# A feed-forward product by seven block products instead of eight, with a separate second product

## The chip, the cores and the metric

The kernel runs on one core of a Trainium2 chip. The core has five engines with queues of their own: TensorE (PE, matmuls; its weight loads are listed apart as PEld), VectorE (DVE), ScalarE (ACT), GpSimd (POOL) and SyncE (SP, which here only issues transfers). Within a queue, instructions start in order; between engines they wait on semaphores. Data lies in DRAM, in SBUF (128 partitions) or in PSUM, where PE accumulates its products in tiles of 128 x 512 float32. The metric is device time in microseconds (us); lower is better.

## The reference

One trunk layer on 1024 tokens of width 1024, in float32: windowed attention heads and gated-DeltaNet heads read one normalised input, their joined output is projected and added to the input, and a feed-forward block with a squared ReLU follows. The change is in the feed-forward part and in the place where it begins:

```python
h = h + jnp.concatenate([attn, gdn], axis=-1) @ w_out[l]
hn = _rmsnorm(h, norm_ffn_w[l])
h = h + jnp.square(jax.nn.relu(hn @ w_ffn_in[l])) @ w_ffn_out[l]
...
return _rmsnorm(h, norm_final_w)
```

`w_ffn_in` is 1024 x 4096 and `w_ffn_out` 4096 x 1024.

## The kernel before

**Arithmetic.** A float32 product is made of three matmuls on rounded halves of the operands. `split` (L112) writes the rounded value h with an ACT cast (L115) and the rest l with a subtraction on POOL (L116). `mm3` (L118) then accumulates h x h, h x l and l x h (L120, L121, L122) into one PSUM tile. Each matmul takes a 128 x 128 stationary block and 512 columns of the moving operand. A `gemm` (L253) runs it over eight blocks of 128 of the contraction: 24 matmuls.

**Buffers.** All SBUF tiles come from tagged pools with a fixed number of buffers: pg (28 of 4 KB per partition), pt (12 of 2 KB), sc and wr (4 each of 4 KB), wh and wl (3 each of 4 KB). PSUM has two tags, psA and psB, of 4 tiles each. A new tile of a tag waits until a buffer of that tag has been read for the last time. The order of each engine's queue is set when the kernel is built, by a planner (`schedule_with_timeline_sim`, L1116) that lists the instructions by their place in the program and by when it expects them to be ready. `weave` (L51) interleaves two generators in the program by the costs that they yield, divided by a weight.

**The stages before the feed-forward part.** Projections, then attention together with the two scans of the DeltaNet, then the output projection. `output` in `phases` (L1068) runs the attention, `out_attn`, the loading of the first group of `w_ffn_in` (`load_w1(0)`, two wr buffers, 512 KB each) and `out_all` (L911), which goes through the eight token chunks from the last to the first. For each chunk, `out_gdn` (L886) takes two wr buffers (`mix` and `zc`), loads the gate with L890, scales (L902), transposes on PE (L905), multiplies (L906) and splits; `out_gemm` multiplies by `w_out` (24 matmuls) and adds to `h[c]` on DVE (L871). h stays in eight pg buffers until the end of the kernel. `norm_h` (L926) makes a chunk's normalised rows in sc buffers (ACT square L199, POOL L186 and L187, DVE L201).

**The feed-forward part.** Tokens are taken in two halves of 512. `hn_half` (L934) transposes a half's rows in eight blocks (four PE transposes each, L205) and splits each block with one ACT instruction (L210) and one DVE instruction (L211) into a pg buffer. The second half is made while the projection ends; the first half beside the first 48 matmuls of `ffn1` on the second half. The hidden features go in 16 groups of 256. For a group, `ffn1` (L957) computes four tiles (two blocks of 128 features, two token halves; 24 matmuls each), with the squared ReLU on ACT and DVE (L964, L965) and a split of the result by ACT and POOL (L966, L967) into pg buffers. `ffn2` (L971) uses these as the stationary operand: for each of eight token chunks and two halves of the output, six matmuls into psB and one DVE addition into h (L983). In the loop of `phases`, `ffn1` of group g + 1 is put ahead of `ffn2` of group g; weights are loaded and split a group ahead (`load_w1` L940, `load_w2` L944). In the last group `finish` (L1000) normalises and stores the rows.

Of the kernel before, what the change touches and what calls it, by code (L numbers as in the profile page):

```python
# [9 lines left out]
F32 = mybir.dt.float32  # L10
# [53 lines left out]
def run(gen):  # L64
    for _ in gen:
        pass
# [7 lines left out]
class Block:  # L74
# [43 lines left out]
    def mm3(self, ps, wh, wl, xh, xl, first, last):  # L118
        nc = self.nc
        nc.tensor.matmul(ps, wh, xh, start=first, stop=False)  # L120
        nc.tensor.matmul(ps, wh, xl, start=False, stop=False)  # L121
        nc.tensor.matmul(ps, wl, xh, start=False, stop=last)  # L122
# [788 lines left out]
    def out_all(self, chunks):  # L911
# [3 lines left out]
        for n, c in enumerate(chunks):  # L915
# [4 lines left out]
            yield from self.out_gemm(self.h[c], *ready.pop(0), self.wo[1])  # L920
            self.summed.append(c)
# [12 lines left out]
    def hn_half(self, half):  # L934
        self.norm_half(half)
        yield 0.5
        self.hnt[half] = []
        yield from self.transpose_split([self.rows[4 * half + i] for i in range(4)], self.w_ffn, "psB", self.hnt[half])

    def load_w1(self, g):  # L940
        raws = self.load_w(self.w_cols(self.io["w_ffn_in"][0], 256 * g, 256))
        return [self.split_w(raws, lambda r: r[:, :, i * P:(i + 1) * P]) for i in range(2)]

    def load_w2(self, g):  # L944
        out = []
        for i in range(2):
            raw = self.wr((P, D))
            r = (2 * g + i) * P
            self.nc.sync.dma_start(out=raw, in_=self.io["w_ffn_out"][0, r:r + P, :])
            h, l = self.sc(dt=F32R), self.sc(dt=F32R)  # L950
# [6 lines left out]
    def ffn1(self, w1, out, order):  # L957

        nc = self.nc
        for i, half in order:  # L960
            a = self.pg((P, 2, HALF), F32R)
            ps = self.gemm(w1[i], self.hnt[half], "psA")
            r, q = self.pt(), self.pt()
            nc.scalar.activation(out=r, in_=ps, func=AF.Relu)  # L964
            nc.vector.scalar_tensor_tensor(out=q, in0=ps, scalar=0.0, in1=r, op0=ALU.max, op1=ALU.mult)  # L965
            nc.scalar.copy(out=a[:, 0], in_=q)  # L966
            nc.gpsimd.tensor_tensor(out=a[:, 1], in0=q, in1=a[:, 0].bitcast(F32), op=ALU.subtract)  # L967
            out[i, half] = a
            yield 5.2

    def ffn2(self, a, w2, tiles, last):  # L971
        nc = self.nc
        for t in tiles:
            tk = slice(t % 4 * P, (t % 4 + 1) * P)
# [3 lines left out]
            for nh, sl in enumerate(halves):  # L978
                ps = self.ps("psB")
                for i in range(2):  # L980
                    at = a[i, t // 4]
                    self.mm3(ps, at[:, 0, tk], at[:, 1, tk], w2[i][0][:, sl], w2[i][1][:, sl], i == 0, i == 1)
# [27 lines left out]
    def build(self):  # L1010
        tc, nc = self.tc, self.nc
        with (
# [6 lines left out]
            self.biasd = d("biasd", (8, 32, 512))[:]  # L1019
            self.gcd = dram.tile([3, 64, P], BF16, name="gcd")[:]  # L1020
# [7 lines left out]
    def phases(self):  # L1028
# [38 lines left out]

        def output():  # L1068
            yield from self.attention()
            yield from self.out_attn()  # L1070
            self.w1 = self.load_w1(0)
# [3 lines left out]
            yield from weave((out, 20.0), (self.hn_half(1), 12.0))  # L1075
# [7 lines left out]
        a, w1 = {}, self.w1  # L1083
        self.norm_half(0)
        run(weave((self.ffn1(w1, a, ((0, 1), (1, 1))), 10.0), (self.hn_half(0), 12.0)))
        run(self.ffn1(w1, a, ((0, 0), (1, 0))))
        w1, w2 = self.load_w1(1), self.load_w2(0)
        for g in range(ng):
            if g + 1 < ng:
                nxt = {}  # L1090
                run(self.ffn1(w1, nxt, ((0, 1), (0, 0), (1, 1), (1, 0))))
                if g + 2 < ng:
                    w1 = self.load_w1(g + 2)
                else:
                    self.w_fin = self.wh((P, D), F32)
                    nc.sync.dma_start(out=self.w_fin, in_=self.io["norm_final_w"].unsqueeze(0).to_broadcast([P, D]))
# [23 lines left out]
```

## Time and profile before

| | |
|---|---|
| median of 3 runs | 1331.63 us (1328.95 to 1333.94) |
| the profiled execution | 1328.63 us |
| its span, first to last instruction | 1326.6 us |
| mean granted TensorE clock | 0.99 |
| transfers | 120.48 MB, mean 91 GB/s |

The profile is of one execution. Busy time is how long an engine had an instruction in flight; for PE, whose matmuls overlap one another, the distance between starts tells the rate and the duration of one matmul doesn't. A row of grouped instructions reads: line, engine, operation, output <- inputs by the names of their buffers, shape, count | busy us, mean ns of one | idle time of the engine before them and what ended it. A row of a stage (A:B, us from the span's start) lists the busy time and the instructions of PE, PEld, DVE, ACT and POOL where these are shown, then the granted clock, the busy share of the DMA engines and GB/s. A row in order of time begins with the start and the duration.

### The profile page before, as it was taken

The numbers are of one execution on the slowest core, as the hardware profiler recorded it, in microseconds if no ns is written. First come the engines' busy times: TensorE is split into PE (matmuls) and PEld (weight loads), VectorE is DVE, ScalarE is ACT, GpSimd is POOL, SyncE is SP. The second block draws the span as 40 slices with busy tenths as digits, with TensorE's granted clock in tenths as the row PEclk, the third lists the DMA queues.
The fourth block names the chain that finished last, engine by engine and source line by source line (L and its number), as shares of the span: only waits on it lengthen the run. The fifth ranks groups of instructions, "written<-read, shape, count | busy, mean of one in ns | idle before, by whom it ended". The sixth has DMA issues, their size and how long they took to land.

```text
span 1326.6 us, 18332 instructions
## 1 busy us (share of the span) xinstructions
PE 1291.2 (97%) x6866; PEld 1041.0 (78%) x6866; DVE 649.7 (49%) x1339; ACT 469.8 (35%) x1085; POOL 460.9 (35%) x432
## 2 busy tenths in 40 slices
PE   7999998999899999999999999999999999999997
PEld 5788876877677778888888888888888888888885
DVE  5667676862689875754223322332233223322336
ACT  6454787244756731235221122112211221122113
POOL 5364122433432251443433133323332333233223
PEclk9999998998899999999999999999999999999999
DMA  6143455315666773120221122012201220122003
GB/s 225 61 133 108 119 174 190 104 48 139 158 173 175 225 284 114 56 72 18 79 64 32 32 64 65 27 37 64 64 19 46 64 64 17 48 64 64 16 1 127
DMA packets 85913, 120.48 MB, mean 91 GB/s; under 512 B 7075, under 2 KB 60448, under 8 KB 85825
## 3 DMA queue, kind: packets, MB, share of 16 engines
q1 hardware_dynamic: 77124, 114.82, 27.2%
q0 software_dynamic: 8448, 4.20, 1.7%
q8 instruction: 54, 0.88, 0.3%
q14 instruction: 34, 0.28, 0.1%
q10 hardware_dynamic: 253, 0.30, 0.1%
HBM read 88.84 MB, written 29.93 MB: 90 GB/s over the span
## 4 chain that ended last, share of the span: by engine, by line
PE 71%; DVE 1%; DMA 0%; issue 0%; ACT 0%; POOLq 0%; POOL 0%; SPq 0%; DVEq 0%; ACTq 0%
PE psA L120 11%; PE psA L121 11%; PE psA L122 11%; PE psB L121 9%; PE psB L120 9%; PE psB L122 9%; PE psB L792 4%; PE psA L580 2%; PE psA L569 1%; PE psA L540 1%; PE psA L541 1%; PE psB L205 0%; DMA pg<-in_w_out 0%; PE psB L756 0%; PE psA L905 0%
## 5 line engine op out<-in xcount | busy, mean ns | idle before, releaser
L120 PE MATMUL psA<-pg,wh 128*128 128x512 f32 x864 | 343.4, 399 | 2.3 <-ACT pt L454 2.1
L121 PE MATMUL psA<-pg,wh 128*128 128x512 f32 x864 | 343.2, 398 | 0.0
L122 PE MATMUL psA<-pg,wl 128*128 128x512 f32 x864 | 343.0, 398 | 0.0
L983 DVE TENSOR_TENSOR pg<-pg,psB 128x512 f32<-128x512 f32 x256 | 175.5, 687 | 277.3 <-PE psB L122 275.9
L116 POOL TENSOR_TENSOR wl<-wr,wh 128x512 fp32r<-128x512 f32 x108 | 152.7, 1435 | 282.4 <-ACT wh L115 282.2
L121 PE MATMUL psB<-sc,pg 128*128 128x512 f32 x512 | 202.5, 396 | 0.0
L120 PE MATMUL psB<-sc,pg 128*128 128x512 f32 x512 | 201.2, 394 | 0.0
L122 PE MATMUL psB<-sc,pg 128*128 128x512 f32 x512 | 200.8, 392 | 0.0
L120 PEld LDWEIGHTS psA<-pg,wh 128*128 128x128 f32 x864 | 163.5, 189 | 41.4 <-ACT pt L454 2.4
L121 PEld LDWEIGHTS psA<-pg,wh 128*128 128x128 f32 x864 | 163.6, 189 | 38.8 <-issue 0.9
L122 PEld LDWEIGHTS psA<-pg,wl 128*128 128x128 f32 x864 | 163.5, 189 | 37.8
L116 POOL TENSOR_TENSOR sc<-wr,sc 128x512 fp32r<-128x512 f32 x64 | 81.7, 1300 | 174.9 <-ACT sc L115 174.9
L965 DVE SCALAR_TENSOR_TENSOR pt<-psA,pt 128x512 f32<-128x512 f32 x64 | 44.0, 689 | 197.5 <-ACT pt L964 197.5
L967 POOL TENSOR_TENSOR pg<-pt,pg 128x512 fp32r<-128x512 f32 x64 | 82.3, 1297 | 157.4 <-ACT pg L966 157.4
L115 ACT CAST wh<-wr 128x512 fp32r<-128x512 f32 x108 | 61.7, 621 | 179.0 <-PE psA L121 154.6
L120 PEld LDWEIGHTS psB<-sc,pg 128*128 128x128 f32 x512 | 96.1, 188 | 23.9 <-ACT sc L115 0.6
L121 PEld LDWEIGHTS psB<-sc,pg 128*128 128x128 f32 x512 | 96.2, 188 | 22.6 <-POOL sc L116 0.5
L122 PEld LDWEIGHTS psB<-sc,pg 128*128 128x128 f32 x512 | 96.0, 188 | 22.3
L115 ACT CAST sc<-wr 128x512 fp32r<-128x512 f32 x64 | 36.4, 618 | 185.3 <-PE psB L121 185.3
L966 ACT CAST pg<-pt 128x512 fp32r<-128x512 f32 x64 | 39.6, 618 | 147.1 <-issue 122.3
L964 ACT ACTIVATE pt<-psA 128x512 f32<-128x512 f32 x64 | 37.8, 593 | 81.1 <-PE psA L122 81.1
L792 PE MATMUL psB<-sc,pg 128*128 128x128 f32 x320 | 47.1, 278 | 1.4 <-DVE sc L805 0.9
(289 smaller groups left out, 1696.2 us busy)
## 6 DMA issues: line engine op xcount, KB each, us to landing
wr<-in_w_ffn_in SPq DMA_DIRECT2D x32, 512.0 KB, 4.7
wr<-in_w_ffn_out SPq DMA_DIRECT2D x32, 512.0 KB, 3.6
wr<-in_w_in SPq DMA_DIRECT2D x22, 512.0 KB, 5.2
pg<-in_x SPq DMA_DIRECT2D x16, 512.0 KB, 5.1
sc<-kvd SPq DMA_DIRECT2D x14, 512.0 KB, 4.4
kvd<-pt SPq DMA_DIRECT2D x16, 256.0 KB, 2.8
atd<-pt SPq DMA_DIRECT2D x16, 256.0 KB, 2.0
pd<-pt SPq DMA_DIRECT2D x16, 256.0 KB, 2.1
```

Source lines behind the costliest of these rows:

```text
L115: nc.scalar.copy(out=h, in_=raw)
L116: nc.gpsimd.tensor_tensor(out=l, in0=raw, in1=h.bitcast(F32), op=ALU.subtract)
L120: nc.tensor.matmul(ps, wh, xh, start=first, stop=False)
L121: nc.tensor.matmul(ps, wh, xl, start=False, stop=False)
L122: nc.tensor.matmul(ps, wl, xh, start=False, stop=last)
L580: nc.tensor.matmul(ps[64 * kv:64 * kv + 64, :], self.va[:, kb, 64 * kv:64 * kv + 64], pts[kv][j].rearrange("p g q -> p (g q)"), start=j == ...
L792: nc.tensor.matmul(ps[:, h - g.start, :], left(h), right[:, h, :], start=True, stop=True)
L964: nc.scalar.activation(out=r, in_=ps, func=AF.Relu)
L965: nc.vector.scalar_tensor_tensor(out=q, in0=ps, scalar=0.0, in1=r, op0=ALU.max, op1=ALU.mult)
L966: nc.scalar.copy(out=a[:, 0], in_=q)
L967: nc.gpsimd.tensor_tensor(out=a[:, 1], in0=q, in1=a[:, 0].bitcast(F32), op=ALU.subtract)
L983: nc.vector.tensor_tensor(out=self.h[t][:, sl], in0=self.h[t][:, sl], in1=ps, op=ALU.add)
```

## The change

The first product is cut in two along three directions: the 256 features of a group into two blocks of 128 (of the weights, A1x and A2x), the contraction into two halves (Ax1 and Ax2 of the weights, B1x and B2x of the activations), and the tokens into the two halves of 512 (Bx1 and Bx2). A group is then a product of 2 x 2 blocks. It is computed with seven block products, P1 to P7, each of 12 matmuls, of sums of blocks: four sums of the weights, S1 to S4, per group on DVE (`columns`), and the sums N1, T2, T3 and N4 of the activations once (`tokens_second`, `tokens_first`). B12 is kept in four pt tiles until the first half is made. The seven operands of four tiles each fill the 28 pg buffers. `pair_products` runs the products of a group; three of them (P6, P3, P4) are accumulated onto the PSUM tile of an earlier one, once that has been read out. For groups 0 and 1, P7 and P3, which need the second token half alone, run ahead in `early`. The squared ReLU is now one DVE instruction (`store_act`), and the activations are stored to DRAM (`ad`), unsplit.

All 16 groups of the first product run ahead of the second product. h is stored to DRAM (`hd`) after the projection and loaded again between the two products. The second product loads the activations and the weights of a group, splits both, and is otherwise the loop over tokens of before, with psA and psB in turn. Removed are `hn_half`, the old `load_w1`, `load_w2` and `ffn1`.

```diff
+    def mm3(self, ps, wh, wl, xh, xl, first, last, onto=False):
+        nc = self.nc
+        nc.tensor.matmul(ps, wh, xh, start=first, stop=False, skip_group_check=onto)
+        nc.tensor.matmul(ps, wh, xl, start=False, stop=False, skip_group_check=onto)
+        nc.tensor.matmul(ps, wl, xh, start=False, stop=last, skip_group_check=onto)
...
             yield from self.out_gemm(self.h[c], *ready.pop(0), self.wo[1])
+            self.nc.sync.dma_start(out=self.hd[c], in_=self.h[c])
             self.summed.append(c)
...
+    def token_block(self, rows, k):
+        ps = self.ps("psB")
+        for i in range(4):
+            self.transpose_row(rows[i], i, ps, k)
+        return ps
+    def operand(self, name, raw, dve):
+        t = self.pg((P, 2, HALF), F32R)
+        self.nc.scalar.copy(out=t[:, 0], in_=raw)
+        (self.nc.vector if dve else self.nc.gpsimd).tensor_tensor(out=t[:, 1], in0=raw, in1=t[:, 0].bitcast(F32),
+                                                                  op=ALU.subtract)
+        self.X[name].append(t)
+    def tokens_second(self):
+        nc = self.nc
+        self.norm_half(1)
         yield 0.5
...
+        rows = [self.rows[4 + i] for i in range(4)]
+        self.b12 = []
+        for k in range(4):
+            ps = self.token_block(rows, k)
+            b12 = self.pt()
+            nc.scalar.activation(out=b12, in_=ps, func=AF.Copy, scale=self.w_ffn[:, k:k + 1])
+            self.b12.append(b12)
+            yield 0.5
+            ps = self.token_block(rows, 4 + k)
+            self.split_rows(ps, self.w_ffn, 4 + k, self.X["B22"])
+            t3 = self.pt()
+            nc.vector.scalar_tensor_tensor(out=t3, in0=ps, scalar=self.w_ffn[:, 4 + k:5 + k], in1=b12, op0=ALU.mult,
+                                           op1=ALU.subtract)
+            self.operand("T3", t3, k % 2)
+            yield 0.5
+    def tokens_first(self):
+        nc = self.nc
+        rows = [self.rows[i] for i in range(4)]
+        w = self.w_ffn
+        for k in range(4):
+            ps = self.token_block(rows, k)
+            self.split_rows(ps, w, k, self.X["B11"])
+            n1, t2, n4 = self.pt(), self.pt(), self.pt()
+            nc.vector.scalar_tensor_tensor(out=n1, in0=ps, scalar=w[:, k:k + 1], in1=self.b12[k], op0=ALU.mult,
+                                           op1=ALU.subtract)
+            yield 0.5
+            b22 = self.X["B22"][k]
+            nc.vector.tensor_tensor(out=t2, in0=n1, in1=b22[:, 0].bitcast(F32), op=ALU.add)
+            nc.vector.tensor_tensor(out=t2, in0=t2, in1=b22[:, 1].bitcast(F32), op=ALU.add)
+            ps = self.token_block(rows, 4 + k)
+            self.split_rows(ps, w, 4 + k, self.X["B21"])
+            nc.vector.scalar_tensor_tensor(out=n4, in0=ps, scalar=w[:, 4 + k:5 + k], in1=t2, op0=ALU.mult,
+                                           op1=ALU.subtract)
+            self.operand("T2", t2, False)
+            self.operand("N1", n1, False)
+            self.operand("N4", n4, True)
+            yield 0.5
     def load_w1(self, g):
...
+        return self.load_w(self.w_cols(self.io["w_ffn_in"][0], 256 * g, 256))
+    PRODUCTS = {"P1": ("A11", "B11", "wh"), "P2": ("A12", "B21", "wl"), "P6": ("S2", "T2", "sc"),
+                "P5": ("S1", "N1", "sc"), "P7": ("S3", "T3", "wh"), "P3": ("S4", "B22", "wl"),
+                "P4": ("A22", "N4", "sc")}
+    def columns(self, raws, names, ops=None):
+        nc = self.nc
+        a = {f"A{i + 1}{kh + 1}": raws[kh][:, :, i * P:(i + 1) * P] for i in range(2) for kh in range(2)}
+        if ops is None:
+            ops = {}
+            mk = lambda: self.pt((P, 4, P))
+            sums = ops["sums"] = {n: mk() for n in ("S1", "S2", "S3", "S4")}
+            v = nc.vector
+            v.tensor_tensor(out=sums["S3"], in0=a["A11"], in1=a["A21"], op=ALU.subtract)
+            v.scalar_tensor_tensor(out=sums["S1"], in0=a["A21"], scalar=-1.0, in1=a["A22"], op0=ALU.mult,
+                                   op1=ALU.subtract)
+            v.scalar_tensor_tensor(out=sums["S2"], in0=sums["S1"], scalar=-1.0, in1=a["A11"], op0=ALU.mult,
+                                   op1=ALU.subtract)
+            v.tensor_tensor(out=sums["S4"], in0=a["A12"], in1=sums["S2"], op=ALU.subtract)
+        for p in names:
+            src, _, tag = self.PRODUCTS[p]
+            raw = a.get(src)
+            raw = ops["sums"][src] if raw is None else raw
+            t = getattr(self, tag)((P, 2, 4, P), F32R)
+            self.split(raw, t[:, 0], t[:, 1])
+            ops[p] = t
+        return ops
+    def product(self, ps, ops, p, first=True):
+        x, o = self.X[self.PRODUCTS[p][1]], ops[p]
+        for k in range(4):
+            self.mm3(ps, o[:, 0, k], o[:, 1, k], x[k][:, 0], x[k][:, 1], first and k == 0, k == 3, not first)
+    def add_to(self, in0, in1):
+        t = self.pt()
+        self.nc.vector.tensor_tensor(out=t, in0=in0, in1=in1, op=ALU.add)
+        return t
+    def copied(self, ps):
+        t = self.pt()
+        self.nc.scalar.copy(out=t, in_=ps)
+        return t
+    def store_act(self, g, i, half, c):
+        self.nc.vector.scalar_tensor_tensor(out=c, in0=c, scalar=0.0, in1=c, op0=ALU.max, op1=ALU.mult)
+        self.nc.sync.dma_start(out=self.ad[2 * g + i, :, half * HALF:(half + 1) * HALF], in_=c)
+    def early(self, ops):
+        d, c = self.ps("psA"), self.ps("psA")
+        self.product(d, ops, "P7")
+        yield 2.8
+        x7 = self.copied(d)
+        self.product(c, ops, "P3")
+        yield 2.8
+        ops["early"] = d, c, x7
+    def pair_products(self, g, ops):
+        tag = "psB" if "early" in ops else ("psA", "psB")[g % 2]
+        a, b = self.ps(tag), self.ps(tag)
+        self.product(a, ops, "P1")
+        p1 = self.copied(a)
+        self.product(b, ops, "P2")
+        self.store_act(g, 0, 0, self.add_to(b, p1))
+        self.product(a, ops, "P6", False)
+        u2 = self.copied(a)
+        c = self.ps(tag)
+        self.product(c, ops, "P5")
+        w = self.add_to(c, u2)
+        if "early" in ops:
+            d, c, x7 = ops["early"]
+            self.store_act(g, 1, 1, self.add_to(w, x7))
+            self.store_act(g, 0, 1, self.add_to(c, w))
+        else:
+            d = self.ps(tag)
+            self.product(d, ops, "P7")
+            self.store_act(g, 1, 1, self.add_to(d, w))
+            self.product(c, ops, "P3", False)
+            self.store_act(g, 0, 1, self.add_to(c, u2))
+        self.product(d, ops, "P4", False)
+        self.store_act(g, 1, 0, self.add_to(d, u2))
+    def load_pair(self, src, mks):
         out = []
         for i in range(2):
             raw = self.wr((P, D))
...
+            self.nc.sync.dma_start(out=raw, in_=src(i))
+            h, l = mks[2 * i](dt=F32R), mks[2 * i + 1](dt=F32R)
             for half in range(2):
                 sl = slice(half * HALF, (half + 1) * HALF)
                 self.split(raw[:, sl], h[:, sl], l[:, sl])
             out.append((h, l))
         return out
...
+    def load_second(self, g):
+        m1, m2 = ((self.wh, self.wl, self.sc, self.wh), (self.wl, self.sc, self.wh, self.wl)) if g == 0 else ((self.pg,) * 4,) * 2
+        a = self.load_pair(lambda i: self.ad[2 * g + i], m1)
+        return a, self.load_pair(lambda i: self.io["w_ffn_out"][0, (2 * g + i) * P:(2 * g + i + 1) * P, :], m2)
     def ffn2(self, a, w2, tiles, last):
         nc = self.nc
         for t in tiles:
...
-                ps = self.ps("psB")
+                ps = self.ps(("psA", "psB")[nh])
                 for i in range(2):
-                    at = a[i, t // 4]
-                    self.mm3(ps, at[:, 0, tk], at[:, 1, tk], w2[i][0][:, sl], w2[i][1][:, sl], i == 0, i == 1)
+                    self.mm3(ps, a[i][0][:, tk], a[i][1][:, tk], w2[i][0][:, sl], w2[i][1][:, sl], i == 0, i == 1)
...
+            self.hd, self.ad = d("hd", (NT, P, D))[:], d("ad", (DFF // P, P, SEQ))[:]
...
+        self.X = {n: [] for n in ("B11", "B21", "B22", "N1", "T2", "T3", "N4")}
+        cols = {}
...
-            self.w1 = self.load_w1(0)
+            cols["raw"] = self.load_w1(0)
+            cols[0] = self.columns(cols["raw"], ("P7", "P3"))
             out = self.out_all(range(NT - 1, -1, -1))
             while len(self.summed) < 6:
                 yield next(out)
-            yield from weave((out, 20.0), (self.hn_half(1), 12.0))
+            yield from weave((out, 20.0), (self.tokens_second(), 12.0))
...
-        a, w1 = {}, self.w1
         self.norm_half(0)
-        run(weave((self.ffn1(w1, a, ((0, 1), (1, 1))), 10.0), (self.hn_half(0), 12.0)))
-        run(self.ffn1(w1, a, ((0, 0), (1, 0))))
-        w1, w2 = self.load_w1(1), self.load_w2(0)
+        raw = self.load_w1(1)
+        cols[1] = self.columns(raw, ("P7", "P3"))
+        run(weave((chain(self.early(cols[0]), self.early(cols[1])), 10.0), (self.tokens_first(), 12.0)))
+        rest = ("P1", "P2", "P6", "P5", "P4")
+        self.columns(cols["raw"], rest, cols[0])
         for g in range(ng):
+            if g == 0:
+                self.columns(raw, rest, cols[1])
+            elif g + 1 < ng:
+                cols[g + 1] = self.columns(self.load_w1(g + 1), ("P1", "P2", "P6", "P5", "P7", "P3", "P4"))
+            else:
+                nxt = self.load_second(0)
+            self.pair_products(g, cols.pop(g))
+        for t in range(NT - 1, -1, -1):
+            self.h[t] = self.pg((P, D))
+            nc.sync.dma_start(out=self.h[t], in_=self.hd[t])
+        for g in range(ng):
+            a, w2 = nxt
             if g + 1 < ng:
-                nxt = {}
-                run(self.ffn1(w1, nxt, ((0, 1), (0, 0), (1, 1), (1, 0))))
-                if g + 2 < ng:
-                    w1 = self.load_w1(g + 2)
-                else:
-                    self.w_fin = self.wh((P, D), F32)
-                    nc.sync.dma_start(out=self.w_fin, in_=self.io["norm_final_w"].unsqueeze(0).to_broadcast([P, D]))
+                nxt = self.load_second(g + 1)
+            else:
+                self.w_fin = self.wh((P, D), F32)
+                nc.sync.dma_start(out=self.w_fin, in_=self.io["norm_final_w"].unsqueeze(0).to_broadcast([P, D]))
             self.ffn2(a, w2, (7, 6, 5, 4, 3, 2, 1, 0), g == ng - 1)
-            if g + 1 < ng:
-                a, w2 = nxt, self.load_w2(g + 1)
```

28 lines of the change are left out of this document (1 added, 27 removed).

## The prediction

> **What bounds the kernel now.** I read the page first: the busy shares and the chain that ended last.
>
> ```profile
> PE 1291.2 (97%) x6866; PEld 1041.0 (78%) x6866; DVE 649.7 (49%) x1339; ACT 469.8 (35%) x1085; POOL 460.9 (35%) x432
> ...
> PE 71%; DVE 1%; DMA 0%; issue 0%; ACT 0%; POOLq 0%; POOL 0%; SPq 0%; DVEq 0%; ACTq 0%
> ```
>
> TensorE (PE) carries the chain, and every other engine is busy half the time or less. A busy share is not yet a rate, so next come the busy times by stage, for the feed-forward part, and the first and the last of 53 matmuls in a row from the order in time.
>
> ```profile
> 700.00:1300.00 600.00, 599.98 (x2585) 485.70 (x2585) 186.94 (x273) 116.35 (x210) 199.70 (x158) 1.00 0.14 43
> ...
> 899.80 0.40 PE L121 MATMUL psA<-pg,wh 128*128 128x512 f32 x1
> ...
> 911.88 0.39 PE L122 MATMUL psA<-pg,wl 128*128 128x512 f32 x1
> ```
>
> 52 steps in 12.08 us: one 128x512 matmul starts every 0.2323 us. The other row agrees: 2585 in 600 us are 0.2321 us each, at granted clock 1.00, with no gap. Both products are in this stretch, in runs of 24 matmuls (first product) and of 6 (second), so changing the PSUM tile costs nothing visible. This stretch is worth its count of matmuls and nothing else.
>
> **What goes.** A group of 256 hidden features needs 96 matmuls in the first product; seven products of 4 x 3 matmuls are 84. 16 groups x 12 = 192 fewer (6866 to 6674), x 0.2323 = **44.6 us**. The second product keeps its 1536, the transposes their 64. What follows can only take away from 44.6.
>
> **The pairs of block columns (16 groups of 84 x 0.2323 = 19.5 us).** What the other engines have to do in that time:
>
> ```profile
> L983 DVE TENSOR_TENSOR pg<-pg,psB 128x512 f32<-128x512 f32 x240 | 165.1, 688 | 272.3 <-PE psB L122 271.0
> ...
> L967 POOL TENSOR_TENSOR pg<-pt,pg 128x512 fp32r<-128x512 f32 x60 | 77.2, 1297 | 150.8 <-ACT pg L966 150.8
> L116 POOL TENSOR_TENSOR sc<-wr,sc 128x512 fp32r<-128x512 f32 x60 | 76.6, 1301 | 167.4 <-ACT sc L115 167.4
> ...
> L115 ACT CAST sc<-wr 128x512 fp32r<-128x512 f32 x60 | 34.1, 617 | 185.3 <-PE psB L121 185.3
> ```
>
> DVE: 4 sums of weights, 5 adds, 4 squared ReLUs, 13 x 0.688 = 8.9 us. POOL: 7 splits x 1.30 = 9.1. ACT: 7 casts and 2 copies x 0.617 = 5.6. All fit in 19.5. They matter through hand-overs: P6 is accumulated onto P1's PSUM tile, after ACT has copied it; P3 onto P5's, after DVE has added it; P4 onto P7's, after DVE has read it. Each time PE has one other product to run first, 12 x 0.2323 = 2.8 us of cover against 0.6 or 0.7 us of reading. What eats cover is the queue in front of the reader, and DVE and POOL get in each other's way:
>
> ```profile
> 562.24 1.30 POOL L116 TENSOR_TENSOR pt<-wr,pt 128x512 fp32r<-128x512 f32 x1 [8.17 <-ACT pt L115]
> ...
> 546.77 0.17 DVE L900 TENSOR_TENSOR sm<-sm,sq 128x4 f32<-128x4 f32 x1
> ...
> 562.43 1.12 DVE L900 TENSOR_TENSOR sm<-sm,sq 128x4 f32<-128x4 f32 x1
> ```
>
> The same tiny DVE instruction took 0.17 us alone and 1.12 us when it met a split on POOL: it ended at 563.55, the split at 563.54. Four sums and four ReLUs of a pair read SBUF twice as L900 does. In the worst case such an instruction waits 1.3, runs 0.69, then the reader's 0.69: 2.7 of 2.8 us, just covered. I take 2 us for all 16 pairs; bounds 0, and 0.7 us (one more DVE instruction in front) x 16 = 11. If the cover were gone altogether, it would be 0.7 us three times a pair: 34 us.
>
> The page "SBUF — State Buffer" of the Trainium skill, section "SBUF: two separate sides", states that VectorE with two SBUF inputs and GpSimd take a shared port pair as an exclusive lock for a whole instruction. The two L900 rows agree to 0.01 us. By that rule alone a pair holds the lock for 8 x 0.69 + 9.1 = 14.6 of 19.5 us, which leaves the time of a pair as it is.
>
> **Queues and transfers.** SP issues, per group, two weight loads and now four stores of 256 KB. A store waits for DVE's square; behind it stand the next weight loads, a group (19.5 us) ahead of use. New in the second product are two 512 KB loads per group beside the two of before, in 96 x 0.2323 = 22.3 us.
>
> ```profile
> 470.00:490.00 20.00, 19.00 (x118) 16.54 (x118) 17.01 (x50) 8.84 (x24) 13.43 (x10) 1.00 0.98 361
> ...
> wr<-in_w_ffn_out SPq DMA_DIRECT2D x32, 512.0 KB, 3.6
> pg<-in_x SPq DMA_DIRECT2D x16, 512.0 KB, 5.1
> ```
>
> 2.1 MB in 22.3 us is 94 GB/s; the trace has 361 GB/s in a stretch. Landing (3.6 us) is far under a group. POOL splits 8 halves, 10.4 of 22.3 us, as many as came before per group at this place and for the activations together. Nothing is added here. Going from the first product to the second costs more: the operands of group 0 go into the buffers wh, wl and sc as the last pair releases them, the last one after P3, 2.8 us before the pair ends, and POOL needs 2.6 us for its two halves; h comes back by eight loads (4.2 MB, at 361 GB/s 12 us) into buffers that come free from P1 on. I take 2 us; bounds 0 (all covered) and 8 (one landing of 5.1 and one tile's split of 2.6, uncovered).
>
> **The last stage before the feed-forward part.** Here the change keeps two of four wr buffers (the raw weights of group 0) until tokens_first is over; out_gdn needs two per chunk. Before, they came free at 535 and two chunks were in flight:
>
> ```profile
> 567.81 0.74 DVE L906 SCALAR_TENSOR_TENSOR wr<-psA,cols,wr 128x512 f32<-128x512 f32 x1
> 568.58 0.36 SPq L890 DMA_DIRECT2D wr<-zd  x1
> DMA to landing us min/median/max: 3.0/3.0/3.5
> ```
>
> The load for a later chunk is issued as L906 releases its buffer: wr already sets this pace. With one chunk in flight the loop is landing 3.0 + L906 0.74 + issue 0.36 = 4.1 us at least; a chunk's projection takes PE 24 x 0.2323 = 5.6 us. So it still fits, without the reserve of a chunk. The eight stores of h wait on SP for a chunk's last add, with later zd loads behind them. I take 2 us; bounds 0 and 12 (1.5 us in each of eight chunks, their difference 5.6 - 4.1, lost).
>
> **The start of the first product.** This is the largest cost. Before, 48 matmuls on the second token half covered hn_half(0), whose DVE work was eight L211. Now four products (P7 and P3 of groups 0 and 1, again 48 matmuls, 11.2 us) cover tokens_first.
>
> ```profile
> 597.11 2.73 DVE L211 SCALAR_TENSOR_TENSOR pg<-psB,cols,pg 128x512 fp32r<-128x512 f32 x4 [1.41 <-ACT pg L210]
> 599.75 0.68 DVE L871 TENSOR_TENSOR pg<-pg,psA 128x512 f32<-128x512 f32 x1
> 607.16 0.75 DVE L201 TENSOR_SCALAR sc<-pg,sm 128x1024 f32<-128x1024 f32 x1
> ...
> 595.91 1.75 PE psB L205 x16
> ...
> 600.00:612.00 12.00, 12.00 (x67) 9.99 (x66) 5.99 (x9) 5.90 (x11) 2.80 (x6) 1.00 0.00 1
> 612.00:624.00 12.00, 11.82 (x64) 9.70 (x63) 6.35 (x10) 7.54 (x14) 2.62 (x3) 1.00 0.01 1
> ```
>
> The last add of the projection (L871) is at 599.75, the last row scaled (L201) at 607.9, first block at DVE about 609.5. Each of four steps now has 7 DVE instructions (two splits, N1, two for T2, N4, its split) at 2.73 / 4 = 0.68 us: 28, 19 us instead of 5.5. P1 needs B11 of the fourth step: 609.5 + 21 x 0.68 + 0.68 = 624.5. PE, from 599.75, has 48 matmuls (11.2), 48 of the 64 transposes at 1.75 / 16 = 0.11 us (5.3) and P1's first nine matmuls (2.1): 618.3. So **6 us** stand open before any meeting with POOL, whose eight splits of T2 and N1 (10.4 us) fall in the same stage, against twelve DVE instructions that read SBUF twice. Half of those waiting 0.5 us adds 3: I take **9 us**. Bounds: 3 (rows finished earlier, fewer meetings) and 18 (each of the twelve waits 1.0 us as L900 did). One pt pool of 12 also holds four b12 tiles and the sums of two groups here; that is inside the upper bound.
>
> A wait of this length also shows in the granted clock elsewhere in the trace:
>
> ```profile
> 317.00:321.00 4.00, 2.02 (x33) 1.00 1.02 236
> 321.00:325.00 4.00, 2.71 (x29) 0.56 0.67 170
> 325.00:329.00 4.00, 4.00 (x16) 0.59 0.90 205
> ```
>
> After 2 us idle the clock was 0.56 to 0.59 for about 8 us, with 16 matmuls in 4 us in place of 17.2: some 0.3 us per 4 us, no term of its own.
>
> **Sum.** -44.6 + 9 (start) + 2 (last stage before) + 2 (pairs) + 2 (between the products) = -29.6 us. The profiled execution took 1328.63 us, 2.03 over its span of 1326.6 and 3.0 under the median of 1331.63. So 1299.0 on its scale, **1302 us** as a median.
>
> **Rivals.**
> (a) Everything is covered: start 3, all else 0, so -41.6, **1290**. For it: the 11.82 of 12 us that PE was busy at 612 to 624. Against it: DVE's 28 instructions.
> (b) The stages around the loop cost their upper bounds: start 18, last stage 12, between 6, pairs 2: -6.6, **1325**, and milder forms down to 1312. For it: wr sets the pace already. Against it: 4.1 us is under 5.6.
> (c) Slower: the hand-overs inside a pair are late each time, because ACT's and DVE's queues hold splits that wait for the buffers of the same pair. Three a pair, 48 in all; -44.6 + 13 leaves 31.6 us to lose, and 0.5% more is 38.3, so it decides from 0.8 us each (more than 3.6 us from product to reader's end). At 1.3 us, one POOL split, it is 62 us: **1362**. Against it: reading takes 0.7 us and cover is 2.8.
> (d) PE doesn't gain what the count says: a change of PSUM tile after every 12 matmuls, each costing one step: 112 x 0.23 = 26 us: **1328**. Against it: runs of 6 and 24 go at one rate.
>
> **Chances.** Forecast (1296 to 1312) 0.56; (a) 0.16; (b) 0.17, of which 0.05 above 1325; (c) 0.07; (d) 0.04. A measurement of this kernel tells about 0.5% (6.7 us) from no change. Faster by over 0.5% (under 1325): 0.56 + 0.16 + 0.12 = 0.84; within: 0.05 + 0.04 = 0.09; slower: 0.07. The range holds the forecast, (a) nearly whole and most of (b): 1289 to 1320; the rest of (b), (c) and (d) lie above.
>
> **What would show it.** PE at 6674 instructions and again one 128x512 matmul per 0.232 us in both products; the groups 19.5 us apart, then 22.3. A gap of 6 to 11 us on PE after the fourth product, ended by a DVE instruction of split_rows: if it is under 3, the start was over-priced; if ended by POOL, my reason is wrong. L906 to L906 below 7 us, else (b). Under 0.2 us of PE waiting per pair, else (c). A matmul step over 0.24 us would bring down the 44.6 itself.

## The result, and the profile after

The change makes the kernel slower: 1370.78 us (median of 4, 1369.67 to 1373.94) against 1330.64 us for the kernel before beside it (4 runs). The ratio is 1.030, with a 95% interval of 1.027 to 1.033. The forecast was 1302 (range 1289 to 1320).

The page of the changed kernel, with the same two lines as before the change (busy times, and the chain that ended last):

```profile
PE 1270.8 (93%) x6674; PEld 1023.7 (75%) x6674; DVE 799.4 (58%) x1505; ACT 485.9 (36%) x1119; POOL 558.1 (41%) x490
...
PE 67%; DVE 9%; ACT 4%; issue 2%; DMA 2%; POOL 2%; POOLq 0%; ACTq 0%; DVEq 0%; SPq 0%
```

The 192 matmuls are gone (6674), but the chain now runs through DVE, ACT and POOL for 15% of the span. The busy times by stage say where; columns as before, the first three stretches in the pairs of block columns, the last in the second product:

```profile
660.00:710.00 50.00, 49.14 (x212) 39.52 (x211) 25.95 (x32) 13.71 (x25) 27.40 (x19) 1.00 0.32 106
710.00:760.00 50.00, 41.80 (x167) 33.00 (x166) 20.88 (x26) 9.96 (x18) 20.65 (x14) 0.93 0.25 84
760.00:810.00 50.00, 41.79 (x158) 32.95 (x157) 20.92 (x26) 8.86 (x16) 19.79 (x14) 0.86 0.25 85
1110.00:1160.00 50.00, 50.00 (x222) 41.44 (x221) 25.14 (x38) 8.54 (x16) 20.09 (x16) 1.00 0.30 94
```

The first pairs go at full rate, and the second product a little above it (222 matmuls in 50 us). From about 710 us on PE idles 8 of 50 us, and the granted clock falls to 0.86 to 0.93. The waits of PE name one kind of instruction (us in total, times, longest):

```profile
PE psB L120 <- ACT sc L115: 26.6, 7, 4.1
PE psA L120 <- ACT sc L115: 21.4, 6, 4.1
```

These are 13 waits, 48.0 us, for the ACT cast of an operand. One of them, of 2.0 us, is at the start; 12 stand in the loop, 46.0 us: eleven of 4.1 us and one of 0.9. In order of time, all engines, one such wait (start, duration, engine, line; in brackets the wait before and what ended it):

```profile
822.75 0.39 PE L122 MATMUL psB<-pg,sc 128*128 128x512 f32 x1
...
823.18 0.69 DVE L1033 TENSOR_TENSOR pt<-psB,pt 128x512 f32<-128x512 f32 x1 [1.38 <-PE psB L122]
...
823.79 0.68 DVE L1010 TENSOR_TENSOR pt<-wr 128x512 f32<-128x512 f32 x1
...
824.39 0.69 DVE L1011 SCALAR_TENSOR_TENSOR pt<-wr,wr 128x512 f32<-128x512 f32 x1
...
824.99 0.69 DVE L1042 SCALAR_TENSOR_TENSOR pt<-pt 128x512 f32<-128x512 f32 x1
...
825.20 1.59 POOL L116 TENSOR_TENSOR wh<-pt,wh 128x512 fp32r<-128x512 f32 x1 [12.15 <-ACT wh L115]
825.60 1.75 DVE L1013 SCALAR_TENSOR_TENSOR pt<-pt,wr 128x512 f32<-128x512 f32 x1
...
827.45 1.14 ACT L115 CAST sc<-pt 128x512 fp32r<-128x512 f32 x2 [1.81 <-DVE pt L1013]
...
828.64 0.80 PE L120 MATMUL psB<-pg,sc 128*128 128x512 f32 x1 [4.10 <-ACT sc L115]
...
829.24 0.63 PE L121 MATMUL psB<-pg,sc 128*128 128x512 f32 x1
...
829.67 0.63 PE L120 MATMUL psB<-pg,wh 128*128 128x512 f32 x1
...
831.80 0.47 PE L122 MATMUL psB<-pg,wh 128*128 128x512 f32 x1
...
832.11 0.40 PE L120 MATMUL psB<-pg,wh 128*128 128x512 f32 x1
```

Read from the first matmul on sc after the wait (828.64) upwards: PE's product P5 waits for the second of two ACT casts into sc (P6's operand S2, then P5's S1). The first of them waits for the DVE sum S2 (L1013). S2 stands behind S3 (L1010) and S1 (L1011), and these start only at 823.79, right behind L1033. That is the last addition of an earlier pair, and it had itself waited for that pair's last matmul, of P4 (822.75). So the sums for a pair's operands don't begin until another pair has ended. What PE has meanwhile, the rest of P2, lasts until 824.5. After the wait, 8 matmuls take 3.47 us (828.64 to 832.11) in place of 8 x 0.2323 = 1.86: 1.6 us more. After the other waits of 4.1 us, 5 to 13 steps from one matmul's start to the next are as slow. All steps over 0.26 us in the loop, the waits left out, are 116, and together they take 23.2 us more than 0.2323 each.

### The profile page after: what moved, and what is told of

The parts are those of the page before. It is cut to its first block, busy times and chain, and to the rows that moved or that the text cites. A ratio compares the mean times of both kernels' runs of the same rounds, so it can differ in the third digit from the quotient of the medians.

```text
span 1368.0 us, 18484 instructions
## 1 busy us (share of the span) xinstructions
PE 1270.8 (93%) x6674; PEld 1023.7 (75%) x6674; DVE 799.4 (58%) x1505; ACT 485.9 (36%) x1119; POOL 558.1 (41%) x490
## 4 chain that ended last, share of the span: by engine, by line
PE 67%; DVE 9%; ACT 4%; issue 2%; DMA 2%; POOL 2%; POOLq 0%; ACTq 0%; DVEq 0%; SPq 0%
PE psA L120 11%; PE psA L121 11%; PE psA L122 11%; PE psB L120 8%; PE psB L121 8%; PE psB L122 8%; PE psB L792 4%; PE psA L580 2%; DVE pt L1013 1%; PE psA L569 1%; ACT sc L115 1%; PE psA L540 1%; DVE pt L1042 1%; DMA ad<-pt 1%; DVE pt L1010 1%
## 5 line engine op out<-in xcount | busy, mean ns | idle before, releaser
L116 POOL TENSOR_TENSOR pg<-wr,pg 128x512 fp32r<-128x512 f32 x120 | 152.2, 1304 | 165.1 <-issue 164.5
L120 PE MATMUL psA<-pg,wh 128*128 128x512 f32 x416 | 172.1, 415 | 2.8 <-ACT pt L454 2.2
L121 PE MATMUL psA<-pg,wh 128*128 128x512 f32 x416 | 170.1, 409 | 0.3 <-POOL pg L945 0.3
L122 PE MATMUL psA<-pg,wl 128*128 128x512 f32 x416 | 167.7, 403 | 0.6 <-POOL wl L116 0.6
L116 POOL TENSOR_TENSOR wl<-wr,wh 128x512 fp32r<-128x512 f32 x48 | 77.2, 1631 | 154.1 <-ACT wh L115 154.0
L1110 DVE TENSOR_TENSOR pg<-pg,psB 128x512 f32<-128x512 f32 x128 | 87.8, 688 | 82.0 <-PE psB L122 82.0
L1110 DVE TENSOR_TENSOR pg<-pg,psA 128x512 f32<-128x512 f32 x128 | 87.7, 687 | 80.3 <-PE psA L122 80.3
L120 PEld LDWEIGHTS psA<-pg,wh 128*128 128x128 f32 x416 | 82.1, 197 | 23.5 <-ACT pt L454 2.4
L121 PEld LDWEIGHTS psA<-pg,wh 128*128 128x128 f32 x416 | 81.9, 197 | 21.0 <-issue 0.9
L122 PEld LDWEIGHTS psA<-pg,wl 128*128 128x128 f32 x416 | 79.6, 191 | 19.6 <-POOL wl L116 1.1
L121 PE MATMUL psA<-pg,pg 128*128 128x512 f32 x240 | 93.5, 390 | 0.0
L120 PE MATMUL psA<-pg,pg 128*128 128x512 f32 x240 | 93.5, 389 | 0.0
L122 PE MATMUL psB<-pg,pg 128*128 128x512 f32 x240 | 93.5, 389 | 0.0
L122 PE MATMUL psA<-pg,pg 128*128 128x512 f32 x240 | 93.4, 389 | 0.0
L120 PE MATMUL psB<-pg,pg 128*128 128x512 f32 x240 | 93.4, 389 | 0.0
L121 PE MATMUL psB<-pg,pg 128*128 128x512 f32 x240 | 93.4, 389 | 0.0
L116 POOL TENSOR_TENSOR wh<-pt,wh 128x512 fp32r<-128x512 f32 x16 | 25.1, 1568 | 151.5 <-ACT wh L115 151.5
L1033 DVE TENSOR_TENSOR pt<-psB,pt 128x512 f32<-128x512 f32 x39 | 27.0, 691 | 101.8 <-ACT pt L1038 49.9
L1033 DVE TENSOR_TENSOR pt<-psA,pt 128x512 f32<-128x512 f32 x39 | 26.8, 691 | 98.4 <-ACT pt L1038 50.0
```

What stands on the lines that cost most here:

```text
L116: nc.gpsimd.tensor_tensor(out=l, in0=raw, in1=h.bitcast(F32), op=ALU.subtract)
L120: nc.tensor.matmul(ps, wh, xh, start=first, stop=False, skip_group_check=onto)
L121: nc.tensor.matmul(ps, wh, xl, start=False, stop=False, skip_group_check=onto)
L122: nc.tensor.matmul(ps, wl, xh, start=False, stop=last, skip_group_check=onto)
L1033: self.nc.vector.tensor_tensor(out=t, in0=in0, in1=in1, op=ALU.add)
L1110: nc.vector.tensor_tensor(out=self.h[t][:, sl], in0=self.h[t][:, sl], in1=ps, op=ALU.add)
```

## Experiments

Two theories come first. **L**: the time goes in the hand-over sum -> cast -> product, because DVE takes the sums late. **B**: the operand is late because its sc buffer comes free late, whatever it is made from. (In the shown wait the ACT cast itself stood 1.81 us until the DVE sum L1013 was there, which speaks for L.) To tell stages apart, the table takes the start of the first and of the last squared ReLU of the pairs on DVE ("loop"). All times are device us; single runs, but for the first, the last and e7.

| kernel | time | before, beside it | first to last squared ReLU | loop |
|---|---|---|---|---|
| the change | 1370.78 | 1330.64 | 648.02 to 1015.11 | 367.1 |
| e1: sums left out | 1294.58 | 1328.57 | 646.58 to 941.38 | 294.8 |
| e2: adds in place | 1312.30 | 1328.57 | 650.26 to 958.55 | 308.3 |
| e5: sums ahead | 1304.53 | 1330.55 | 651.21 to 951.09 | 299.9 |
| e8: e2 and e5 | 1298.16 | 1331.51 | 650.16 to 943.15 | 293.0 |
| e10: e5, one group ahead | 1302.12 | 1331.51 | 645.46 to 947.89 | 302.4 |
| e12: e8 and e10 | 1295.66 | 1329.41 | 644.68 to 939.55 | 294.9 |

**e1, without the sums.** The four sums of weights are left out: the products take blocks of the raw weights instead.

```diff
-            sums = ops["sums"] = {n: mk() for n in ("S1", "S2", "S3", "S4")}
...
+            ops["sums"] = {"S1": a["A21"], "S2": a["A11"], "S3": a["A21"], "S4": a["A12"]}
```

> The four sums of weights S1 to S4 are left out: P5, P6, P7 and P3 take raw blocks of the weights in their place. Theory L (late sums: in DVE's queue the sums of a group stand behind the last add of the pair two before, so that PE waits 13 times for the cast of P5's operand, 48 us in all, and each such wait is followed by some 2 us of a lower clock): the waits go, 1371 - 48 - 26 = 1297 us (1285 to 1312). Rival B (the operand is late because its sc buffer comes free late, whatever it is made from): above 1350 us, the waits on ACT sc L115 stay.

1294.58 us. Two stretches of its pairs (PE alone, clock, DMA share, GB/s):

```profile
710.00:760.00 50.00, 50.00 (x217) 1.00 0.32 105
760.00:810.00 50.00, 50.00 (x217) 1.00 0.29 97
```

No gap, clock 1.00, and over the whole loop 1268 matmuls in 294.8 us, 0.2325 us each. The sc buffers are the same, so B falls; this supports L, and the rate of PE in the pairs is as forecast. But it takes away the sums' place in the queue and their work at once.

**e2, adds in place.** Both works stay. The additions write onto one of their inputs, so a pair takes four new pt tiles instead of seven, and the last addition takes none.

```diff
-    def add_to(self, in0, in1):
-        t = self.pt()
+    def add_to(self, in0, in1, t=None):
+        t = self.pt() if t is None else t
...
-            self.store_act(g, 1, 1, self.add_to(d, w))
+            self.store_act(g, 1, 1, self.add_to(d, w, w))
...
-        self.store_act(g, 1, 0, self.add_to(d, u2))
+        self.store_act(g, 1, 0, self.add_to(d, u2, u2))
```

> The adds of a pair write onto one of their inputs, so that a pair needs four pt tiles in place of seven; in DVE's queue two of the four sums then stand ahead of the pair's last add and no longer behind it. Theory L: the sums come one product (2.8 us) earlier, the 13 waits of 3.7 us shrink to about 1, the clock does not drop: 1371 - 13 x (2.8 + 2) = 1309 us (1290 to 1330). Rival B: 1371 within 8 us.

1312.30 us: 58 less for the same arithmetic. The sums now stand in DVE's queue behind the pair's fourth addition, the last one that takes a new tile. Eight waits on this cast are left in the loop, 10.3 us in all.

**e3, one more pt buffer** (`self.buf("pt", 13, ...)` in place of 12).

> One pt buffer more (13 in place of 12); the order of DVE's queue in the pairs stays as it is. Theory L: no change, 1371 within 6 us, since the sums stand behind the same add. Rival P (the sums wait for their own pt buffer to come free): over 20 us faster.

1375.01 us: nothing gained, and the waits are as in the change. So it isn't the number of pt buffers.

**e4, another order of operands.** P4's operand, which needs no sum, is split third, ahead of P6's.

```diff
-                cols[g + 1] = self.columns(self.load_w1(g + 1), ("P1", "P2", "P6", "P5", "P7", "P3", "P4"))
+                cols[g + 1] = self.columns(self.load_w1(g + 1), ("P1", "P2", "P4", "P6", "P5", "P7", "P3"))
```

> The operand of P4 is split third and not last, so that the raw weights (wr) and the sc buffers change hands in another order; DVE's queue in the pairs stays as it is. Theory L: no change, 1371 within 8 us. Rival B (sc and wr buffers set when the operands are there): over 20 us faster or slower.

1357.51 us. Neither band was hit: it is 13 us faster, and the 12 waits moved to ACT's copies (L1038), ten of 3.0 us and two of 1.9. In ACT's queue the copy stands behind the cast of S2, and the sums still start right behind the addition after P4 (at 796.09, the addition at 795.48). The order of the splits shifts where PE waits; it doesn't take the cause away.

**e5, the sums ahead.** If the cause is the place of the sums in the program, it is enough to write them earlier. The loading of the weights and the four sums of group g + 2 move into pair g, behind the addition after P5; the splits stay where they were.

```diff
+        between()
         if "early" in ops:
...
+                self.columns(cols[g + 1]["raws"], ("P1", "P2", "P6", "P5", "P7", "P3", "P4"), cols[g + 1])
...
+            def between():
+                if g + 2 < ng:
+                    cols[g + 2] = self.columns(self.load_w1(g + 2), ())
```

> The sums of group g + 2 are written in the program inside pair g, behind P5's add, and no longer behind the whole pair; the arithmetic and the buffers are those of the change. In DVE's queue they now stand two adds and three squares earlier. Theory L, with its cause (the pt buffers are given out in program order, so that a sum can't be placed ahead of the add that takes the pair's last pt tile): all 13 waits and the low clock go, 1371 - 74 = 1297 us (1288 to 1312). Rival N (e1 was fast because the sums' DVE time and their meetings with POOL were gone): the 8.9 us of DVE per pair stay, so above 1330 us.

1304.53 us: 66 less, with as many instructions on PE, DVE, ACT and POOL as in the change. N falls. The loads of the weights moved too, but in the change no sum of the loop waits for a load: each S3 starts right behind an addition, as at 823.79. DVE in order of time:

```profile
789.45 0.69 DVE L1034 TENSOR_TENSOR pt<-psB,pt 128x512 f32<-128x512 f32 x1 [4.19 <-ACT pt L1039]
790.06 0.73 DVE L1010 TENSOR_TENSOR pt<-wr 128x512 f32<-128x512 f32 x1
790.71 0.68 DVE L1011 SCALAR_TENSOR_TENSOR pt<-wr,wr 128x512 f32<-128x512 f32 x1
791.43 0.69 DVE L1013 SCALAR_TENSOR_TENSOR pt<-pt,wr 128x512 f32<-128x512 f32 x1
792.22 1.60 DVE L1015 TENSOR_TENSOR pt<-wr,pt 128x512 f32<-128x512 f32 x1
793.75 0.68 DVE L1034 TENSOR_TENSOR pt<-psB,pt 128x512 f32<-128x512 f32 x1
```

The sums stand between two additions of one pair, behind one before which DVE had sat idle 4.19 us, and are ready a pair ahead. All waits of PE from 645 to 960 (the one on POOL comes behind the loop, at 952):

```profile
PE psA L121 <- POOL wl L116: 1.1, 1, 1.1
PE psB L120 <- ACT sc L115: 1.0, 4, 0.2
PE psA L120 <- ACT sc L115: 0.7, 3, 0.2
```

46 us of waiting on the cast have become 1.7. e2, e3 and e5 fit one reading: DVE's queue follows the program where a sum takes a new pt tile, since the tiles of a tag are handed out in that order; a sum can't pass the addition that took the last tile before it. That the place of the sums in the queue is the cause is shown; why the planner put them there is this reading, and no run tests the planner itself.

**e6, the start.** The four steps of `tokens_first` are cut in two loops (B11 and N1 first, N1 in place of b12), and groups 0 and 1 run P5 ahead of P2.

```diff
+            n1 = self.b12[k]
...
+            self.operand("N1", n1, False)
             yield 0.5
+        for k in range(4):
+            n1, t2, n4 = self.b12[k], self.pt(), self.pt()
...
-        rest = ("P1", "P2", "P6", "P5", "P4")
+        rest = ("P1", "P5", "P2", "P6", "P4")
```

> Only the start: tokens_first makes B11 and N1 for all four steps first and then B21, T2 and N4, N1 in place of b12; in groups 0 and 1 P5 runs ahead of P2. The same DVE instructions. The late sums stay. Theory S (PE waits 13.8 us at 600 to 640, since P1 needs the fourth step of 28 DVE instructions): P1 and P5 of two groups, 11 us more of cover, fill most of it, 1371 - 10 = 1361 us (1355 to 1366), PE busy at 600 to 650 up by 8 us or more. Rival Q (the start waits for POOL and the pt buffers): 1371 within 4 us.

1371.76 us: no gain, so this theory of the start falls. Q's number came true; its mechanism is not tested by that.

**e7, e5 and e6 together.**

> e5 and e6 together. Theories L and S, added up: 1297 - 10 = 1287 us (1280 to 1300), 0.967 of the kernel before. If the two share a cause, as only one of the gains: 1293 to 1300.

1305.11 us (4 runs, 1303.94 to 1305.97), ratio 0.981 (0.979 to 0.982): outside both bands and e5's time again, so e6's edit gains nothing with the late sums gone either.

**e8, adds in place and sums ahead** (the edits of e2 and e5).

> The sums ahead (e5) and the adds in place (e2) in one kernel. From the first to the last squared ReLU of the pairs, e1 (no sums) takes 294.8 us, e5 299.9: 5 us of the loop are still open. If they are left over from the handing out of pt buffers, four tiles fewer per pair give most of them back: 1300 us (1298 to 1302), and the loop in 296. If they are the sums' own time on DVE and their meetings with POOL, nothing changes: 1304.5 +- 2 and a loop of 300.

1298.16 us and a loop of 293.0: no wait of PE between 660 and 960 is left. The window holds 1260 matmuls, 0.2325 us each, as in e1, so the sums' own work costs PE nothing that shows.

The next three try the start again, in the order of `tokens_first` and in what is put ahead of it. They are single runs, and runs of one kernel here lie 2 to 5 us apart (e7, e12, the change, the kernel before), so their times alone decide little; the traces say more.

**e9, another order of the start.**

```diff
             ps = self.token_block(rows, 4 + k)
             self.split_rows(ps, w, 4 + k, self.X["B21"])
+            b22 = self.X["B22"][k]
+            t2, n4 = self.pt(), self.pt()
...
+            for t in late:
+                self.operand(*t)
+            late = [("N1", n1, False), ("T2", t2, False), ("N4", n4, True)]
```

> e5 with the four steps of the start written in another order: both splits of a step ahead of its combinations, and the three operand splits one step later, N1 in place of b12. Theory C (at the start ACT and DVE wait for each other: ACT's cast of an operand stands in front of the next block's scaling, so each step takes 6 to 7 us where its seven DVE instructions are 4.8): four steps save some 1.8 us each, 1297 us (1295 to 1300), the idle time of PE from 600 to 640 falls from 13.6 us to 7 or less. Rival R (the start is set by when the first block can begin: rows and the sums of group 1 ahead of it on DVE, until 619): 1304.5 +- 2.

1307.36 us, 2.8 over e5 and just above R's band, and PE still idles 12.3 us from 600 to 640, where C had 7 or less: C falls. The waits in PE's stream only moved:

```profile
629.59 1.11 PE L205 MATMUL psB<-ident,sc 128*128 128x128 f32 x4 [2.47 <-DVE pt L987]
...
635.23 1.08 PE L205 MATMUL psB<-ident,sc 128*128 128x128 f32 x4 [4.53 <-DVE pt L980]
```

**e10, only group 0 ahead of the first tokens.**

```diff
-        cols[1] = self.columns(raw, ("P7", "P3"))
-        run(weave((chain(self.early(cols[0]), self.early(cols[1])), 10.0), (self.tokens_first(), 12.0)))
+        run(weave((self.early(cols[0]), 10.0), (self.tokens_first(), 12.0)))
...
+        cols[1] = self.columns(raw, ())
```

> e5 with only group 0's P7 and P3 ahead of the first tokens; the sums and products of group 1 come behind them. This takes four sums (4.9 us of DVE with the long ones) and two casts out of the way of the first block, and 24 matmuls (5.6 us) out of PE's cover. If the sums set when the first block begins (R), it begins 5 us earlier and the two cancel: 1304.5 +- 2, the first split of B11 at 617 or before. If the steps alone set the pace (C alone), the cover is missing: 1310 (1308 to 1312).

1302.12 us. DVE in order of time, the first split of B11:

```profile
613.97 0.75 DVE L211 SCALAR_TENSOR_TENSOR pg<-psB,cols,pg 128x512 fp32r<-128x512 f32 x1 [1.26 <-ACT pg L210]
```

It starts at 613.97 and in e5 at 622.32, 8.3 us earlier; the kernel gains only 2.4, 0.4 beyond R's band and no more than single runs differ by. PE's idle time from 600 to the first squared ReLU stays, 12.3 us against 13.4, as 24 matmuls of cover (5.6 us) went with the sums. R fits best: the sums of group 1 on DVE hold back the first block, and moving them trades wait for cover. What the rows alone set no run tests.

**e11, e9 and e10 together.**

> The edits of e9 and e10 together. If both theories hold, the first block begins 5 us earlier, the steps take 4.8 us, and 24 matmuls more stand behind: 1297 to 1300, as e9. If only R holds: 1304.5 +- 2. If only C: 1303 (5.6 over e9).

1304.79 us: in the band of R alone.

**e12, the best parts together** (e2, e5 and e10).

> e8 and the edit of e10 in one kernel: sums ahead, adds in place, and only group 0's P7 and P3 ahead of the first tokens. If the two are independent, e8's 1298.2 less the 2.4 us of e10 against e5: 1296 (1293 to 1299). If the start only moved its wait, 1298 as e8.

1295.66 us (1294.57 to 1297.15, 4 runs; before 1329.41, 7 runs), ratio 0.975 (0.974 to 0.977). This computes what the change computes and beats both kernels. What e10's edit adds to e8 stays open: 2.5 us against a single run is the spread of e12's own runs. Its stages, all engines, start and pairs:

```profile
600.00:660.00 60.00, 47.63 (x200) 35.91 (x199) 50.43 (x60) 29.38 (x54) 40.46 (x31) 0.86 0.18 57
660.00:710.00 50.00, 50.00 (x217) 40.46 (x216) 37.16 (x40) 14.35 (x25) 30.55 (x21) 1.00 0.39 129
710.00:760.00 50.00, 50.00 (x216) 40.45 (x216) 30.60 (x34) 13.52 (x23) 24.82 (x18) 1.00 0.34 110
```

## Why the prediction was wrong

**What goes, 44.6 us: right.** The 192 matmuls are gone, and in e1, e8 and e12 the pairs run without a gap at 0.232 to 0.233 us per matmul.

**The stages around the loop: right in sum, partly by luck.** The span grew by 1368.0 - 1326.6 = 41.4 us. With 44.6 gained and 72.3 lost in the loop (the change's loop less e1's), 13.7 us are lost around it. The prediction had 9 + 2 + 2 = 13. But the start cost about twice its 9 us, and a gain that the sum didn't hold made up for it.
- The start. From 600 to 640, PE in the changed kernel (busy us, count, clock, DMA share, GB/s):

```profile
600.00:610.00 10.00, 8.25 (x42) 1.00 0.13 53
610.00:620.00 10.00, 7.18 (x34) 1.00 0.35 102
620.00:630.00 10.00, 3.63 (x19) 0.86 0.01 4
630.00:640.00 10.00, 7.13 (x22) 0.63 0.06 14
```

  13.8 us idle, and a lower clock behind it; 9 was forecast, 18 the bound. From 600 to the first squared ReLU at 648 PE starts 100 matmuls and 45 transposes; at 0.2323 and 0.11 us these are 28 us, so about 20 of the 48 are lost. The gap is in pieces, about half of it ended by DVE's combinations (L979, L987) and none by `split_rows`. DVE as the main cause was right, its count was not: the first block was to reach DVE at 609.5, and its split starts at 619.13. Ahead of it stand the four sums of group 1 (609.19 to 616.8, two of them 1.75 and 1.76 us long beside POOL) and the rows between them; the forecast counted these sums only as buffers. The steps then take 6.9 us each, where it had seven instructions, 4.8 us.
- The second product made up for it. Its matmuls start 0.2267 us apart (882 in the 200 us from 1100 to 1300), and not 0.2323 as in both products before and as forecast. Over 1536 matmuls this gains 8.6 us. Why it is faster no run shows.
- The last stage before cost nothing: L871 ends it at 599.93, before the change at 599.75. The sign named for (b), L906 to L906 over 7 us, was badly chosen: the longest step is 9.2 us (553.09 to 562.25), but before the change there was one of 9.4 (551.32 to 560.76).
- Between the products PE waits once, 2.2 us, for a split on POOL (L116 into wl): 2 was forecast.

**The pairs: the step that failed.** "They matter through hand-overs" went on to count only one kind: the reading of a PSUM tile before the next product is accumulated onto it. "I take 2 us for all 16 pairs; bounds 0, and 0.7 us [...] x 16 = 11." The term measures 72.3 us, 367.1 - 294.8, the change's loop less e1's. Nothing in the sum followed an operand from its sum on DVE through the cast on ACT to its product. That DVE's 8.9 us "fit in 19.5" was true, and DVE is busy only 58% of the span, but its sums stood behind an addition that waits for the last product of the pair two before. What was said of the weight loads, "a group (19.5 us) ahead of use", held for them, and not for the sums made from them.

Of the 72.3 us the 12 waits take 46.0 and the slower steps behind them 23.2. The rest is 12 x 0.17 = 2 us, by which a step with a wait is longer than the wait and a usual step, and 0.9 us for four more matmuls in the window (1272 against 1268). So the late sums account for all of it. e5's remaining 5.1 us over e1 are seven waits (1.7), the longer steps at them (1.9) and six more matmuls in its window (1.4).

**Rival (c)** gave 1362, nearest to the result, and its test ("under 0.2 us of PE waiting per pair, else (c)") pointed the right way. That its number came so near is luck, for its mechanism was another: it had splits wait for buffers of their own pair, 48 times 1.3 us. The splits here wait for data (the cast at 827.45 for L1013), and one pt buffer more changed nothing (e3). At 0.07 it had too small a chance, because the argument against it ("reading takes 0.7 us and cover is 2.8") looked at one hand-over out of two.

**The clock** was put off as "no term of its own", at some 0.3 us per 4 us. That misread its row: the 16 matmuls at 325 to 329 include small ones of 64x64 (L756), and the 128x512 ones that follow start 0.43 us apart (326.11, 326.54, 326.96). The idle stretch ahead of them was 3.27 us and not 2. Eleven waits of 4.1 us each brought such a stretch, and they cost 23.2 us.

**The port.** The sum L1013 took 0.69 us in e5, at 791.43, and 1.75 at 825.60, where it met POOL's split: it ended at 827.35, the split at 826.79. This is the meeting that the L900 rows showed ahead of the change, where 0.95 us was lost. All its 16 instances in the changed kernel (ns min/median/max), and who waited for them:

```profile
L1013 DVE SCALAR_TENSOR_TENSOR pt<-pt,wr x16: 679/1750/1783, 520.0 to 980.7; 128x512 f32<-128x512 f32 x16
...
who waited for it (us, times):
  ACT sc L115: 29.4, 14
```

The meeting adds about 1 us to a chain that was already on the path; the place in the queue puts it there. In e12 L1013 still takes 1.19 us in the median and up to 1.78, and PE doesn't wait in the loop.

## What to carry to other kernels

Follow each operand of a product back through every engine that makes it, and ask at each what stands in front of it in the queue and what that waits for; a busy share that fits says nothing of this. When sums, casts and products of successive steps share one tag of buffers, write the production of the next step ahead of the last use in this one, or let results overwrite an input: here the same arithmetic went from 1370.8 to 1295.7 us by order and placement alone. An edit that only moves a producer out of the way, as e10 does at the start, can take away nearly as much cover as it saves.

## What the hardware showed that was not expected

Whether a wait costs clock is not settled by its length alone, and the drop can come late. The waits named here, of several runs, each follow a stretch of PE at full rate. After waits of 0.9 to 1.4 us (e2) the next matmuls stay 0.23 us apart. Around 2 us both happen: after 1.91 and 1.95 us (e4) and 2.10 us (e11) at least six steps of 0.43 us follow; after 1.90 (e10), 2.14 (e9), 2.24 (the change) and 2.72 us (e6) none does. In e4 ten of the 12 waits on the copies are 3.0 us, and each is followed by 5 to 13 such steps, at once or up to about 1 us after PE has resumed (e4, PE in order of time):

```profile
753.36 0.80 PE L120 MATMUL psB<-pg,sc 128*128 128x512 f32 x1 [3.03 <-ACT pt L1038]
753.95 0.63 PE L121 MATMUL psB<-pg,sc 128*128 128x512 f32 x1
...
803.12 0.50 PE L120 MATMUL psB<-pg,sc 128*128 128x512 f32 x1 [3.03 <-ACT pt L1038]
803.46 0.40 PE L121 MATMUL psB<-pg,sc 128*128 128x512 f32 x1
...
804.21 0.63 PE L121 MATMUL psB<-pg,sc 128*128 128x512 f32 x1
804.64 0.63 PE L122 MATMUL psB<-pg,sc 128*128 128x512 f32 x1
```

In the first place the step right after the wait is 0.59 us and five of 0.43 follow; in the second the steps are 0.34, 0.24, 0.23 and 0.29, and seven of 0.43 follow from 804.21 on; then the step is 0.23 again. So a shorter wait isn't safe by being a little shorter; of those up to 1.4 us none cost clock here.

The page "TensorE: Matmul & The Clock Gate" of the Trainium skill, section "HAM oscillation — how this bites in real kernels", names gaps of more than about 3.4 us as those after which PE falls to half clock. The changed kernel's waits of 4.1 us agree with it; the 3.0 us in e4, and three waits of about 2 us, already showed the drop, so here the measurement goes below the page's figure.
